# GpSimd issues the modulation loads, ScalarE the two small loads of the time mixing

## The chip, the cores and the metric

The kernel runs on one core of one Trainium2 chip. The metric is the device time of one execution in microseconds (us), and the median of several executions is compared. The core has five engines with instruction streams of their own, each executed in order: TensorE (PE, with its weight loads shown as PEld), VectorE (DVE), ScalarE (ACT), GpSimd (POOL) and SyncE (SP). SyncE computes nothing here. It only issues transfers (DMAs), each of which waits in SyncE's queue until the buffer it writes is free.

## The reference

The reference is a two-layer network on one sequence of 256 tokens with 2048 features, all in float32. Layer 0 mixes over time with an RWKV-7 recurrence, and layer 1 with chunked attention over shared keys and values. Both end in a squared-ReLU MLP with 8192 hidden features. Each sub-layer's shift, scale and gate are a product of one conditioning vector `c` with a large matrix:

```python
for layer in range(DEPTH):                                  # DEPTH = 2
    mod = c @ w_ada[layer] + b_ada[layer]                   # (1, 2048) @ (2048, 12288)
    sh1, sc1, gt1, sh2, sc2, gt2 = jnp.split(mod, 6, axis=-1)
    if layer == N_A_LAYERS:                                 # layer 1: the shared keys and values
        sh_kv, sc_kv = jnp.split(c @ w_ada_kv + b_ada_kv, 2, axis=-1)
        h_kv = modulate(rms_norm(x, g_kv), sh_kv, sc_kv)
        ...
    h = modulate(rms_norm(x, g_mix[layer]), sh1, sc1)
    y = rwkv7_time_mix(h, ...) if layer < N_A_LAYERS else chunk_band_attention(h, kp, vp, ...)
    x = x + gt1[:, None, :] * y
    h = modulate(rms_norm(x, g_mlp[layer]), sh2, sc2)
    x = x + gt2[:, None, :] * sq_relu_mlp(h, w_up[layer], w_down[layer])
return rms_norm(x, g_final)
```

Inside the time mixing, decay, in-context rate and gate come from low-rank products, whose second factors are the arrays the kernel calls `lora2`.

## The kernel before

**Weights.** Every large weight matrix is streamed from HBM in tiles of 128 x 1024 float32 (512 KB), into the rotating buffer `raw` (6 deep). For each tile `halves` writes `wH`, a rounded copy, on ScalarE (L378) and `wL`, the rest, on VectorE (L381), both 3 deep. TensorE multiplies with both halves (`proj2`, L412 and L413). One output tile of 128 features takes two `raw` tiles and 32 matmuls; below it is called a step. An MLP has 64 steps of `w_up` (activations `aHL`) and 64 of `w_down` (activations `hHL`), in four rounds of 16 and 16.

**Modulation.** The products with `c` are made on VectorE beside the matrix work: `ada_load` loads a 512 KB tile of the transposed matrix `w_ada_t`, and `ada_step` multiplies it with `c`, held in `cb`, and sums along the row (L459). Inside the MLPs and the attention the tile comes from a pool of its own, the buffer `rada`; `ada_room(n)` opens that pool, with n = 5 in an MLP and n = 3 in the attention. Everywhere else, in the time mixing above all, it is a `raw` buffer. 273 of these tiles are `rada` and 111 are `raw`. They all are used up by the end of the attention's output projection, so that the MLP of layer 1 has none.

**Time mixing.** The heads are taken as 16 pairs. The steps of up to five pairs are interleaved with the projections of the next (`proj_steps`, L819 and on). Each pair loads two small tiles, `lw` (L829, 96 KB) and `lg` (L277, 128 KB), into one buffer each.

**Who sets the order.** The program is recorded in source order, and then a scheduler arranges each engine's instructions: it may put an instruction ahead of earlier ones whose inputs are not there yet. That order is fixed when the program is built, and on the chip every engine follows its own in order. So the issuing engine of a load decides behind what else the load waits, and the built order of other engines may change with it.

Of the kernel before, what the change touches and what calls it, by code (L numbers as in the profile page):

```python
# [77 lines left out]
class Pair:  # L78
# [13 lines left out]
    def s(self, name="s", bufs=8):  # L92
        return self.b.pw.tile([P, T], F32, tag=name, bufs=bufs, name=name)
# [4 lines left out]
    @staticmethod  # L98
    def ch(t):
        return t.rearrange("p (c t) -> p c t", t=C)  # L100
# [165 lines left out]
    def late(self):  # L266
        b, nc, j, s, ch, v = self.b, self.b.nc, self.j, self.s, self.ch, self.v
        kr, ar, mk, bk, vp, u, pc, heads = self.kr, self.ar, self.mk, self.bk, self.vp, self.u, self.pc, self.heads
        pw, pp, mm = b.pw, b.pp, nc.tensor.matmul

        bank = pp.tile([P, 2, T], F32, tag="lt", bufs=2, name="lt")
        pch, py = bank[:, 0, 0:3 * C].rearrange("p (a t) -> p a t", a=3), bank[:, 1, :]
        zs = None
        for c in range(4):
            if c == 3:
                lg = pw.tile([P, 2, P], F32, tag="lg", bufs=1, name="lg")
                nc.sync.dma_start(out=lg, in_=b.d["lora2"][j, :, 2:4])  # L277
            g, sa = (pw.tile([P, C], F32, tag=n_, bufs=3, name=n_) for n_ in ("g", "sa"))
            for K in heads:
                mm(pch[K, 0, :], mk[K, c, 0:C], vp[K, c, :], start=True, stop=(c == 0))  # L280
            if c:
                for K in heads:
                    mm(pch[K, 0, :], kr[K, c, 0:C], zs[K, :], start=False, stop=True)
            nc.scalar.copy(g, pch[:, 0, :])
            yield
            for K in heads:
                mm(pch[K, 1, :], u[K, c, :], g[K, :], start=True, stop=True)
            nc.scalar.mul(sa, pch[:, 1, :], -1.0)
            yield
            for K in heads:  # L290
                mm(ch(py)[K, c, :], vp[K, c, :], mk[K, c, C:P], start=True, stop=False)
            if c:
                for K in heads:
                    mm(ch(py)[K, c, :], zs[K, :], kr[K, c, C:P], start=False, stop=False)
            for K in heads:
                ins = mm(ch(py)[K, c, :], sa[K, :], ch(ar)[K, c, :], start=False, stop=True)
            if c < 3:
                with b.tc.issue_after(ins.ins):
                    for K in heads:
                        mm(pch[K, 2, :], bk[K, 0, c, :], sa[K, :], start=True, stop=False)  # L300
                    for K in heads:
                        mm(pch[K, 2, :], bk[K, 1, c, :], vp[K, c, :], start=False, stop=True)
                zn = pw.tile([P, C], F32, tag="zs", bufs=4, name="zs")
                if c == 0:
                    nc.vector.tensor_copy(zn, pch[:, 2, :])
                else:
                    nc.vector.scalar_tensor_tensor(out=zn, in0=zs, scalar=pc[:, c, :], in1=pch[:, 2, :],
                                                   op0=ALU.mult, op1=ALU.add)
                zs = zn
            yield  # L310

        sq = self.square(py)
        yield
        var = b.psm()[:, :T]
        self.head_sums(var, sq)
        yield
        rg = s("sl", 1)
        nc.scalar.activation(rg, var, AF.Ln, scale=1.0 / C, bias=b.col(C_GN))
        nc.scalar.activation(rg, rg, AF.Exp, scale=-0.5)
        nc.vector.scalar_tensor_tensor(out=rg, in0=py, scalar=b.vec("ln_w", j), in1=rg, op0=ALU.mult, op1=ALU.mult)  # L320
        yield
        pg = b.psm()[:, :T]
        for i in range(2):
            mm(pg, lg[:, i, :], self.tg[:, i, :], start=(i == 0), stop=(i == 1))  # L324
        nc.vector.scalar_tensor_tensor(out=rg, in0=v, scalar=b.vec("ln_b", j), in1=rg, op0=ALU.add, op1=ALU.add)
        nc.vector.tensor_tensor(out=v, in0=pg, in1=rg, op=ALU.mult)
        yield


class Body:  # L330
# [27 lines left out]
            self.ada_pool = None  # L358

    def raw(self, src, shape=None, ada=False):  # L360
        if ada and self.ada_pool:
            pool, n = self.ada_pool
            t = pool.tile([P, HK * P], F32, tag="rada", bufs=n, name="rada")
        else:
            t = self.wp.tile([P, HK * P], F32, tag="raw", bufs=self.RAW_BUFS, name="raw")
        if shape is not None:
            t = t.rearrange("p (a b) -> p a b", a=shape)
        self.nc.sync.dma_start(out=t, in_=src)
        return t

    def halves(self, raw, lo=0):

        nc = self.nc
        H = self.wp.tile([P, HK, P], F32R, tag="wH", bufs=self.W_BUFS, name="wH")
        L = self.wp.tile([P, HK, P], F32R, tag="wL", bufs=self.W_BUFS, name="wL")
        Hf, Lf = (t.rearrange("p a b -> p (a b)")[:, lo:] for t in (H, L))
        raw = raw[:, lo:]
        nc.scalar.copy(Hf, raw)  # L378
        self.nhalf += 1
        eng = nc.gpsimd if self.pool_every and self.nhalf % self.pool_every == 0 else nc.vector  # L380
        eng.tensor_tensor(out=Lf, in0=raw, in1=Hf, op=ALU.subtract)  # L381
        return H, L
# [239 lines left out]
    def layer_a(self, st, sp):  # L622
        nc, tc, d = self.nc, self.tc, self.d
# [5 lines left out]
        with ExitStack() as s1:  # L629
# [9 lines left out]
            for q in range(4):  # L639
                (nc.sync if q % 2 else nc.scalar).dma_start(out=h[:, 4 * q:4 * q + 4, 1:T + 1],  # L640
                                                            in_=d["x"][:, 4 * q:4 * q + 4, :])
# [79 lines left out]
            def mixed(m, n, xx):  # L721
                t = ph.tile([P, T], F32, tag="mix", bufs=4, name="mix")
                nc.vector.scalar_tensor_tensor(out=t, in0=xx, scalar=self.vec(f"mu{m}", n),  # L723
                                               in1=h[:, n, 1:T + 1], op0=ALU.mult, op1=ALU.add)
                return t
# [26 lines left out]
            for n in range(KT):  # L752
# [19 lines left out]
                t = mixed(5, n, xx)  # L772
# [33 lines left out]
        with ExitStack() as s1:  # L806
# [12 lines left out]
            def proj_steps(pr):  # L819
                for dst, hl in (("k", xk), ("r", xr)):  # L820
                    w = self.wnext
                    src = next(weights, None)
                    self.wnext = None if src is None else self.weight(src)
                    ps = pp.tile([P, 2, T], F32, tag="pj", bufs=2, name="pj")
                    for kt in range(KT):
                        self.proj2(ps, w, lambda kt: hl[:, kt, :, 0:T], (kt, kt + 1))
                        if dst == "r" and kt == 1:
                            pr.lw = pw.tile([96, 2, P], F32, tag="lw", bufs=1, name="lw")
                            nc.sync.dma_start(out=pr.lw, in_=d["lora2"][pr.j, :96, 0:2])  # L829
                        if kt % 2 == 1:  # L830
                            if kt == KT - 1:
                                t = pw.tile([P, T], F32, tag=dst, bufs=2, name=dst)
                                nc.scalar.copy(t, ps[:, 0, :])
                                nc.vector.tensor_tensor(out=t, in0=ps[:, 1, :], in1=t, op=ALU.add)
                                setattr(pr, dst, t)
                            yield
# [363 lines left out]
```

## Time and profile before

| | us |
|---|---|
| median of 3 executions | 2736.1 (2728.79 to 2736.61) |
| the profiled execution | 2743.32 |
| its span in the trace | 2741.5 |
| layer 0, up to the time mixing | 0 to 190 |
| time mixing | 190 to 730 |
| its output projection (`out_proj`, `w_o`) | 730 to 792.5 |
| MLP of layer 0 | 792.5 to 1574.5 |
| attention and its output projection | 1574.5 to 2003.5 |
| MLP of layer 1, then the final norm | 2003.5 to 2741.5 |

The borders of the stages are the starts of the first matmuls of each (rounded for the first two). A row of a profile view names the line of the program, the engine, the instruction, what it writes and reads with buffer numbers left out, and times in us or ns. The letter q behind an engine's name marks its queue of transfers. `DVE wL L381 <- ACT wH L378` in the list of waits means that VectorE stood idle before line 381 until ScalarE had finished line 378.

### The profile page before, as it was taken

What the parts mean: (1) busy time and instruction counts of PE and PEld (TensorE: products, weight loads), DVE (VectorE), ACT (ScalarE), POOL (GpSimd) and SP (SyncE); (2) the same over time, 40 slices, a digit from 0 to 9 for tenths busy, and PEclk for the clock granted to TensorE, in tenths of its full rate; (3) what the DMA queues carried; (4) which work ended last, traced back from release to release, by engine and by line L of the source; (5) the groups of instructions that cost most, each with busy time, mean ns of one, the idle gap of its engine ahead of it and who ended that gap; (6) DMA issues with size and microseconds to landing.
All of it is one profiled execution on the core that took longest, in us unless ns stands there. A gap on an engine that the chain in (4) does not pass through costs nothing.

```text
span 2741.5 us, 55497 instructions
## 1 busy us (share of the span) xinstructions
PE 2611.7 (95%) x22154; PEld 2220.0 (81%) x22154; DVE 2093.3 (76%) x3493; ACT 1333.7 (49%) x2432; POOL 199.4 (7%) x320
## 2 busy tenths in 40 slices
PE   6998999999999999999999989999999999999997
PEld 3777777777889878887878788877898888888886
DVE  5778888889789777888878998797985555556555
ACT  3345545545446335345345454466455354453554
POOL 0002322222100000000000100000100000000002
PEclk9999999999999999999999999999999999999999
DMA  9966556566688888888888878885865555555553
GB/s 337 313 230 210 197 179 201 187 199 230 218 297 274 301 297 304 306 320 305 307 294 302 294 265 297 325 293 173 296 205 186 187 189 186 189 187 186 188 189 123
DMA packets 219251, 669.27 MB, mean 244 GB/s; under 512 B 21616, under 2 KB 69104, under 8 KB 218992
## 3 DMA queue, kind: packets, MB, share of 16 engines
q1 hardware_dynamic: 216928, 663.18, 71.4%
q8 instruction: 174, 2.85, 0.4%
q10 hardware_dynamic: 2064, 2.54, 0.3%
q14 instruction: 85, 0.70, 0.1%
HBM read 663.54 MB, written 2.10 MB: 243 GB/s over the span
## 4 chain that ended last, share of the span: by engine, by line
PE 59%; DMA 17%; DVE 14%; issue 6%; ACT 2%; SPq 0%; POOL 0%; DVEq 0%; ACTq 0%; POOLq 0%
PE pj L412 31%; PE pj L413 16%; DMA rada<-w_ada_t 10%; DVE wL L381 6%; DMA raw<-w_ada_t 5%; DVE raw L459 2%; DVE rada L459 2%; PE pj L403 1%; PE pj L401 1%; PE pj L402 1%; ACT wH L378 1%; DMA raw<-w_up 1%; PE ms L324 1%; DVE mix L723 0%; PE iv L111 0%
## 5 line engine op out<-in xcount | busy, mean ns | idle before, releaser
L412 PE MATMUL pj<-aHL,wH 128*128 128x512 f32 x3328 | 1205.0, 403 | 1.1 <-DVE v L750 0.9
L381 DVE TENSOR_TENSOR wL<-raw,wH 128x1024 fp32r<-128x1024 f32 x772 | 942.5, 1222 | 302.2 <-ACT wH L378 300.0
L378 ACT CAST wH<-raw 128x1024 fp32r<-128x1024 f32 x772 | 804.7, 1045 | 701.1 <-PE pj L412 601.3
L413 PE MATMUL pj<-aHL,wL 128*128 128x256 f32 x3328 | 940.5, 283 | 13.0 <-DVE wL L381 12.5
L412 PEld LDWEIGHTS pj<-aHL,wH 128*128 128x128 f32 x3328 | 630.5, 189 | 153.3 <-issue 9.3
L412 PE MATMUL pj<-hHL,wH 128*128 128x512 f32 x2048 | 729.0, 400 | 10.1 <-DVE hHL L963 10.1
L413 PEld LDWEIGHTS pj<-aHL,wL 128*128 128x128 f32 x3328 | 630.4, 189 | 25.7 <-DVE wL L381 23.8
L413 PE MATMUL pj<-hHL,wL 128*128 128x256 f32 x2048 | 578.6, 283 | 8.5 <-DVE wL L381 8.3
L412 PEld LDWEIGHTS pj<-hHL,wH 128*128 128x128 f32 x2048 | 387.7, 189 | 105.3 <-DVE hHL L963 11.4
L459 DVE SCALAR_TENSOR_TENSOR rada<-rada,cb 128x1024 f32<-128x1024 f32 x273 | 333.2, 1223 | 130.9 <-DMA rada<-w_ada_t 114.4
L413 PEld LDWEIGHTS pj<-hHL,wL 128*128 128x128 f32 x2048 | 389.8, 190 | 15.2 <-DVE wL L381 14.6
L509 POOL TENSOR_TENSOR ss<-ss,sq 128x256 f32<-128x256 f32 x56 | 49.4, 882 | 1642.6 <-ACT sq L508 1642.4
L988 DVE SCALAR_TENSOR_TENSOR x<-pj,mod,x 128x256 f32<-128x256 f32 x256 | 123.4, 482 | 54.5 <-PE pj L413 51.5
L459 DVE SCALAR_TENSOR_TENSOR raw<-raw,cb 128x1024 f32<-128x1024 f32 x111 | 137.9, 1247 | 29.9 <-DMA raw<-w_ada_t 29.3
L960 ACT ACTIVATE t<-t 128x256 f32<-128x256 f32 x112 | 47.0, 420 | 221.5 <-DVE t L932 221.5
L401 PE MATMUL pj<-aHL,wH 128*128 128x258 f32 x384 | 111.1, 289 | 7.1 <-DVE ks L556 4.8
L403 PE MATMUL pj<-aHL,wL 128*128 128x258 f32 x384 | 110.1, 287 | 2.7 <-DVE wL L381 2.7
L402 PE MATMUL pj<-aHL,wH 128*128 128x258 f32 x384 | 110.7, 288 | 0.0
L401 PEld LDWEIGHTS pj<-aHL,wH 128*128 128x128 f32 x384 | 74.2, 193 | 7.9 <-issue 6.0
L403 PEld LDWEIGHTS pj<-aHL,wL 128*128 128x128 f32 x384 | 75.1, 196 | 3.6 <-DVE wL L381 3.3
L402 PEld LDWEIGHTS pj<-aHL,wH 128*128 128x128 f32 x384 | 74.6, 194 | 0.1
L961 ACT ACTIVATE hHL<-t 128x256 fp32r<-128x256 f32 x128 | 53.0, 414 | 5.0 <-DVE t L556 4.5
(240 smaller groups left out, 2789.7 us busy)
## 6 DMA issues: line engine op xcount, KB each, us to landing
rada<-w_ada_t SPq DMA_DIRECT2D x273, 512.0 KB, 6.3
raw<-w_up SPq DMA_DIRECT2D x256, 512.0 KB, 4.6
raw<-w_down SPq DMA_DIRECT2D x256, 512.0 KB, 4.6
raw<-w_ada_t SPq DMA_DIRECT2D x111, 512.0 KB, 4.5
rawa<-w_ada SPq DMA_DIRECT2D x64, 512.0 KB, 7.0
raw<-w_k SPq DMA_DIRECT2D x32, 512.0 KB, 3.7
raw<-w_r SPq DMA_DIRECT2D x32, 512.0 KB, 5.1
raw<-w_o SPq DMA_DIRECT2D x32, 512.0 KB, 5.1
```

What stands on the lines that cost most here:

```text
L378: nc.scalar.copy(Hf, raw)
L381: eng.tensor_tensor(out=Lf, in0=raw, in1=Hf, op=ALU.subtract)
L401: nc.tensor.matmul(ps, H[:, i, :], a(kt)[:, 0, :], start=(first and kt == 0), stop=False)
L402: nc.tensor.matmul(ps, H[:, i, :], a(kt)[:, 1, :], start=False, stop=False)
L403: ins = nc.tensor.matmul(ps, L[:, i, :], a(kt)[:, 0, :], start=False, stop=(last and kt == KT - 1))
L412: nc.tensor.matmul(ps, H[:, i, :], a(kt), start=(kt == 0), stop=False)
L413: ins = nc.tensor.matmul(ps[:, 0, :], L[:, i, :], a(kt)[:, 0, :], start=False, stop=(kt == KT - 1))
L459: nc.vector.scalar_tensor_tensor(out=raw, in0=raw, scalar=1.0, in1=self.cb, op0=ALU.mult, op1=ALU.mult, accum_out=sums[:, n:n + 1])
L509: (eng or nc.gpsimd).tensor_tensor(out=self.ss, in0=self.ss, in1=sq, op=ALU.add)
L960: nc.scalar.activation(t, t, AF.Relu)
L961: nc.scalar.activation(h[:, 0, :], t, AF.Square)
L988: nc.vector.scalar_tensor_tensor(out=x, in0=ps[:, i, :], scalar=self.mods[(layer, 5)][:, n:n + 1], in1=x, op0=ALU.mult, op1=ALU.add)
```

## The change

Three calls change the engine that issues a transfer. `raw` keeps SyncE for weight tiles, and takes GpSimd for a tile of the pool `rada`. `lw` and `lg` are issued by ScalarE. No transfer is added, left out or changed in size, and no buffer changes.

```diff
@@ class Pair, late(): the fourth chunk
             if c == 3:
                 lg = pw.tile([P, 2, P], F32, tag="lg", bufs=1, name="lg")
-                nc.sync.dma_start(out=lg, in_=b.d["lora2"][j, :, 2:4])
+                nc.scalar.dma_start(out=lg, in_=b.d["lora2"][j, :, 2:4])
@@ class Body, raw()
     def raw(self, src, shape=None, ada=False):
+        queue = self.nc.sync
         if ada and self.ada_pool:
             pool, n = self.ada_pool
+            queue = self.nc.gpsimd
             t = pool.tile([P, HK * P], F32, tag="rada", bufs=n, name="rada")
         else:
             t = self.wp.tile([P, HK * P], F32, tag="raw", bufs=self.RAW_BUFS, name="raw")
...
-        self.nc.sync.dma_start(out=t, in_=src)
+        queue.dma_start(out=t, in_=src)
@@ class Body, layer_a(), proj_steps()
                             pr.lw = pw.tile([96, 2, P], F32, tag="lw", bufs=1, name="lw")
-                            nc.sync.dma_start(out=pr.lw, in_=d["lora2"][pr.j, :96, 0:2])
+                            nc.scalar.dma_start(out=pr.lw, in_=d["lora2"][pr.j, :96, 0:2])
```

The changed program is two lines longer from `raw` on, so L368, L378, L381 and L459 of before are L370, L380, L383 and L461 after.

The built order changes in three places. First SyncE, in the MLP of layer 0, where the `w_down` of one round gives way to the `w_up` of the next; before:

```order
L368 DMA raw<-w_down 128x1024 x3
L368 DMA rada<-w_ada_t 128x1024
L368 DMA raw<-w_down 128x1024
L368 DMA rada<-w_ada_t 128x1024
L368 DMA raw<-w_up 128x1024
L368 DMA rada<-w_ada_t 128x1024
L368 DMA raw<-w_up 128x1024 x2
```

After, over the first round and a half:

```order
L370 DMA raw<-w_up 128x1024 x32
L370 DMA raw<-w_down 128x1024 x3
L449 DMA cb<-c_row 128x1024
L370 DMA raw<-w_down 128x1024 x29
L370 DMA raw<-w_up 128x1024 x2
L449 DMA cb<-c_row 128x1024
L370 DMA raw<-w_up 128x1024 x30
```

Between the weight tiles no `rada` tile is left, only a reload of `cb` now and then.

Second GpSimd, from the end of the time mixing to the attention; `ss` is the running sum of squares of the next norm, and the memsets of `s` belong to the attention's scores. Before:

```order
L249 COPY uf_2236<-u 32x4x32 x4
L249 COPY uf_2237<-u 32x4x32 x4
L509 TENSOR_TENSOR ss<-ss,sq 128x256 x28
L1067 MEMSET s 64x64
L1068 MEMSET s 64x64
```

After (the first 14 `ss` belong to the output projection of the time mixing, the next 14 to the end of the MLP of layer 0):

```order
L370 DMA rada<-w_ada_t 128x1024 x3
L511 TENSOR_TENSOR ss<-ss,sq 128x256
L370 DMA rada<-w_ada_t 128x1024 x2
L511 TENSOR_TENSOR ss<-ss,sq 128x256
L370 DMA rada<-w_ada_t 128x1024 x2
L511 TENSOR_TENSOR ss<-ss,sq 128x256
L370 DMA rada<-w_ada_t 128x1024
L511 TENSOR_TENSOR ss<-ss,sq 128x256
L370 DMA rada<-w_ada_t 128x1024 x2
L511 TENSOR_TENSOR ss<-ss,sq 128x256
L370 DMA rada<-w_ada_t 128x1024 x231
L511 TENSOR_TENSOR ss<-ss,sq 128x256
```

The loads stand between GpSimd's sums, and 231 of them follow each other through most of the MLP of layer 0. 253 of the 273 now stand ahead of the attention's first scores.

Third VectorE, in the `w_up` of the last round of the same MLP; `t` and `hHL` are the activations of a step. Before:

```order
L459 TENSOR_SCALAR rada,ada_sums<-rada,cb 128x1024
L381 TENSOR_TENSOR wL<-raw,wH 128x1024
L963 TENSOR_TENSOR hHL<-t,hHL 128x256
L381 TENSOR_TENSOR wL<-raw,wH 128x1024
L932 TENSOR_TENSOR t<-pj,t 128x256
L459 TENSOR_SCALAR rada,ada_sums<-rada,cb 128x1024
L381 TENSOR_TENSOR wL<-raw,wH 128x1024
L963 TENSOR_TENSOR hHL<-t,hHL 128x256
L459 TENSOR_SCALAR rada,ada_sums<-rada,cb 128x1024
L381 TENSOR_TENSOR wL<-raw,wH 128x1024
```

After:

```order
L383 TENSOR_TENSOR wL<-raw,wH 128x1024
L461 TENSOR_SCALAR rada,ada_sums<-rada,cb 128x1024
L965 TENSOR_TENSOR hHL<-t,hHL 128x256
L383 TENSOR_TENSOR wL<-raw,wH 128x1024
L461 TENSOR_SCALAR rada,ada_sums<-rada,cb 128x1024
L934 TENSOR_TENSOR t<-pj,t 128x256
L383 TENSOR_TENSOR wL<-raw,wH 128x1024
L461 TENSOR_SCALAR rada,ada_sums<-rada,cb 128x1024
L965 TENSOR_TENSOR hHL<-t,hHL 128x256
L383 TENSOR_TENSOR wL<-raw,wH 128x1024
```

Here every `wL` has a modulation product beside it, where before about three of four had one. Counted over the whole order, the products up to the first late norm of this MLP (L555, after: L557) are 12 before and 17 after, up to the first residual add of the last round (L988, after: L990) 170 and 241, and up to its end 192 and 253. On TensorE 80 rows of 17,671 change place.

## The prediction

> **What bounds the kernel now.** I read the busy times by stage first, because the two MLPs do the same matrix work, 128 steps each, and only the first carries modulation tiles. The columns are span, then busy time and instructions of each engine, the granted TensorE clock, the share of time the 16 DMA engines were busy, and GB/s.
>
> ```profile
> 792.50:1574.50 782.00, 744.25 (x4229) 642.39 (x4228) 645.52 (x960) 364.55 (x548) 11.93 (x15) 0.99 0.86 300
> 1574.50:2003.50 429.00, 417.74 (x2565) 353.58 (x2563) 372.59 (x681) 222.52 (x426) 17.27 (x77) 1.00 0.79 275
> 2003.50:2729.10 725.60, 723.22 (x4227) 634.79 (x4228) 433.46 (x561) 370.21 (x548) 16.02 (x15) 1.00 0.57 182
> 190.00:730.00 540.00, 505.30 (x9330) 419.23 (x9330) 450.92 (x931) 278.64 (x750) 124.58 (x178) 0.98 0.61 197
> ```
>
> The MLP of layer 1 runs at TensorE's pace: 723 of 726 us busy. The same matmuls take 782 us in layer 0. These 56 us are the most that this stage can give. The attention leaves TensorE 11 us idle. Next I read who waits in the MLP of layer 0 (total us, times, longest).
>
> ```profile
> DVE rada L459 <- DMA rada<-w_ada_t: 86.0, 73, 3.2
> PEld pj L413 <- DVE wL L381: 35.5, 50, 2.4
> DVE wL L381 <- ACT wH L378: 29.5, 36, 1.6
> ```
>
> VectorE waits 86 us for modulation tiles, and the `wL` behind them in its order come late for TensorE. Busy time and these two waits make 645 + 86 + 30 = 761 of the 782 us: VectorE's chain sets this stage. Why the tiles are late shows in the timeline (start, duration), SyncE's queue first.
>
> ```profile
> 968.48 0.42 SPq L368 DMA_DIRECT2D rada<-w_ada_t  x1
> 972.78 3.06 SPq L368 DMA_DIRECT2D raw<-w_up  x2
> 975.90 0.42 SPq L368 DMA_DIRECT2D rada<-w_ada_t  x1
> ...
> 960.66 1.23 DVE L459 SCALAR_TENSOR_TENSOR rada<-rada,cb 128x1024 f32<-128x1024 f32 x1
> 963.78 1.23 DVE L459 SCALAR_TENSOR_TENSOR rada<-rada,cb 128x1024 f32<-128x1024 f32 x1 [0.74 <-DMA rada<-w_ada_t]
> 969.99 1.23 DVE L459 SCALAR_TENSOR_TENSOR rada<-rada,cb 128x1024 f32<-128x1024 f32 x1 [1.92 <-DMA rada<-w_ada_t]
> 973.12 1.23 DVE L459 SCALAR_TENSOR_TENSOR rada<-rada,cb 128x1024 f32<-128x1024 f32 x1
> 975.65 1.23 DVE L459 SCALAR_TENSOR_TENSOR rada<-rada,cb 128x1024 f32<-128x1024 f32 x1 [0.16 <-DMA rada<-w_ada_t]
> 983.09 1.23 DVE L459 SCALAR_TENSOR_TENSOR rada<-rada,cb 128x1024 f32<-128x1024 f32 x1 [2.83 <-DMA rada<-w_ada_t]
> 984.64 1.22 DVE L381 TENSOR_TENSOR wL<-raw,wH 128x1024 fp32r<-128x1024 f32 x1
> ...
> 985.91 0.39 PE L413 MATMUL pj<-hHL,wL 128*128 128x256 f32 x1 [1.53 <-DVE wL L381]
> ```
>
> The product at 983.09 waited 2.83 us for the load of 975.90. That load writes one of five buffers, and the product five places back had left it at 961.9 (960.66 + 1.23). For 14 us it stood behind two weight loads that waited for buffers of their own. The `wL` at 984.64 was late by that, and TensorE stood 1.53 us.
>
> **The change part by part.** *The queue of the modulation tiles.* GpSimd does next to nothing in this stage (11.9 of 782 us), so a load can now go out as soon as its buffer is free.
>
> ```profile
> L368 SPq DMA_DIRECT2D rada<-w_ada_t x273: 327/424/1089, 756.1 to 1993.7; - x137
> L459 DVE SCALAR_TENSOR_TENSOR rada<-rada,cb x273: 1205/1224/1693, 762.3 to 2000.2; 128x1024 f32<-128x1024 f32 x137
> DMA to landing us min/median/max: 4.0/6.3/8.8
> ```
>
> In the example that is 21 us ahead (983.09 − 961.9), against 4.0 to 8.8 us to landing. If nothing else changed, the 86 us of waits would go, and nearly all of the 56 us with them.
>
> *The built order.* But the scheduler uses the freedom. By the order, the products inside this MLP rise from 180 (192 less 12) to 236 (253 less 17), and 224 of them stand ahead of the last `w_down` round, where 158 did. That is 66 more in the first seven eighths, and 12 instead of 22 in the last. The attention loses them. So I take the seven eighths apart: 684 us before (7/8 of 782), and 635 at TensorE's pace (7/8 of 725.6). VectorE: 565 busy (7/8 of 645.5), plus 66 x 1.22 = 81, makes 646, and with its wait for `wH` (7/8 of 29.5 = 26) 672 us. DMA: 205 MB (7/8 of 300 GB/s x 782 us) plus 66 x 0.524 MB = 240 MB. The rates which this chip reached with such tiles are:
>
> ```profile
> 1700.00:1800.00 100.00, 97.44 (x571) 82.73 (x570) 80.80 (x128) 47.32 (x80) 0.46 (x4) 1.00 0.88 320
> 1690.00:1700.00 10.00, 9.82 (x59) 8.42 (x58) 6.95 (x11) 4.55 (x8) 0.00 (x0) 1.00 0.96 342
> 1760.00:1770.00 10.00, 10.00 (x60) 8.76 (x59) 7.71 (x12) 4.35 (x7) 0.00 (x0) 1.00 0.99 379
> ```
>
> 320 GB/s over 100 us gives 750 us, 342 at share 0.96 gives 702, 379 at 0.99 gives 633. With its own queue full at all times the rate should lie between the last two; I take 355, which gives 676. VectorE's 672 and the DMA's 676 both stand above TensorE's 635, so 676: **−8 us**, with ends at −38 (VectorE's 646 without a wait) and +66.
>
> The last eighth has few products: 97.8 to TensorE's 90.7, **−7**. The products fetched forward from the attention use its three buffers instead of five. There a tile takes at least (6.3 landing + 1.22 product + 0.42 issue)/3 = 2.65 us, and the 37 of the last `w_up` round 98 us, against 97 of the 676 that fall on that round: **+1**. With 8.8 us to landing it would be 3.48 us each, 129 us, +32; I take the median, since nothing but their own kind is queued ahead of them.
>
> *The attention* has 72 products before and 20 after.
>
> ```profile
> DVE rada L459 <- DMA rada<-w_ada_t: 28.3, 25, 4.5
> ```
>
> Most of this wait goes, but TensorE was idle for only 11.3 us there, which is the upper end; the lower is zero. I take half, **−6**.
>
> *The output projection before the MLP* has 5 more products by the order (17 for 12), 5 x 1.22 = 6 us of VectorE; some of it lies beside TensorE's work: **+2** of 0 to +6.
>
> *The time mixing.* ScalarE takes over 32 loads.
>
> ```profile
> 0.77 0.43 ACTq L575 DMA_DIRECT2D ct<-c  x1
> SPq L277 <- PE lt L287: 15.5, 8, 5.4
> SPq L829 <- PE ms L128: 4.1, 5, 1.1
> DVE raw L459 <- DMA raw<-w_ada_t: 29.3, 32, 2.6
> ```
>
> The first row is what an issue costs ScalarE: 0.43 x 32 = 13.8 us of its queue, beside 279 busy of 540, so part of it is hidden by idle time; each stands ahead of small copies on which the pair's next matmuls wait. In return SyncE no longer holds weight and modulation loads behind `lg` and `lw` for 20 us, of which VectorE's 29.3 us of waits could give some back. Ends −13 and +14; I take **+3**, nearer to zero because both sides lie beside other work.
>
> Sum: −8 −7 +1 −6 +2 +3 = −15. The profiled execution took 2743.3 us (span 2741.5), so it would take 2728.3; it lies 7.2 above the median of the three timed runs, 2736.1, and on that footing the forecast is **2721 us**. About 0.3%, 8 us, is what a measurement of this kernel can tell from no change.
>
> **The rivals.** *Transfers bind (slower).* The seven eighths turn from a gain to a loss that eats the other −7 where the 240 MB come at less than 347 GB/s (240/691). Between 345 and 320 GB/s they take 695 to 750 us, and the sum is +4 to +59; in the middle +30, or 2766 us. For it: 320 is the best that any 100 us of this kind of work has shown, and the products now stand between every two `wL`, so each late tile stops TensorE's weights. Against it: so far SyncE's queue, not the engines, held the loads back.
>
> *GpSimd's issuing holds up VectorE (slower).* A row shows that the two engines can collide.
>
> ```profile
> 778.64 1.22 DVE L381 TENSOR_TENSOR wL<-raw,wH 128x1024 fp32r<-128x1024 f32 x1
> 781.30 1.77 DVE L381 TENSOR_TENSOR wL<-raw,wH 128x1024 fp32r<-128x1024 f32 x1
> 781.25 0.74 POOL L509 TENSOR_TENSOR ss<-ss,sq 128x256 f32<-128x256 f32 x1 [8.13 <-ACT sq L508]
> ```
>
> Beside a GpSimd sum the same operation took 0.55 us longer. If each load's issue did that, 224 x 0.55 = 123 us would lie on VectorE's 672, and the kernel would come to about 2840. It decides from (691 − 672)/224 = 0.08 us a load. No trace here has a load from GpSimd, so this price runs from zero to 0.55; I take zero, since the sum reads and writes whole tiles of 128 x 256, which an issue does not. The Trainium skill (SBUF — State Buffer, "Who interferes with whom") says that a VectorE instruction with two SBUF inputs collides with a GpSimd instruction that reads SBUF, and infers that making descriptors needs only the write side. The row agrees with the first half; by the second this rival's price is zero too.
>
> *No change.* The wait moves from the queue to the transfer: at about 347 GB/s the stage stays at its 782 us and the rest cancels, 2736. The Trainium skill (DMA: Bandwidth & Descriptors, "Issuing engines are not separate DMA queues") says that starting DMAs on several engines saves only the sequencer's time to start them. By that the change would save SyncE's 273 x 0.424 = 116 us, which are on no path. The trace speaks against it with the 14 us in which the load at 975.90 was held by order alone.
>
> *All the waits go.* At 379 GB/s and with `wH` in time, VectorE's 646 sets the seven eighths, 30 below what I take: 2691.
>
> **How the numbers follow.** Forecast 0.33, all waits gone 0.13, no change 0.14, transfers bind 0.25, VectorE held up 0.15. Faster by over 0.3%: 0.46, within: 0.14, slower: 0.40. The forecast's own range is 2700 to 2727. The whole range starts at 2688, just past the case without waits, and ends at 2785, which takes in most of the binding transfers (to 2795) and the small end of the holding-up; beyond it are some 0.15 above and 0.04 below.
>
> **What would show it.** In the trace of after, the MLP of layer 0 should take 760 to 778 us at 338 to 348 GB/s, with VectorE near 715 us busy there; VectorE's waits for `rada` should fall well below 86 us in spite of 56 more products, and a load should go out within a microsecond of the product that frees its buffer. The attention should take 420 to 427 us, the time mixing 540 to 545. A row of L383 with a mean above 1.25 us in the MLP would speak for the holding-up, waits for `rada` above 86 us at a DMA share over 0.95 for the binding transfers. The reasoning is wrong if the stage gets faster though the waits stay, or if the tiles land later than 8.8 us while the DMA engines stand idle.

## The result and the profile after

| | before | after |
|---|---|---|
| median of 4 executions, us | 2736.36 (2728.79 to 2736.65) | 2713.77 (2709.22 to 2717.43) |
| ratio, 95% interval | | 0.9923 [0.9900, 0.9946] |
| the profiled execution (its span), us | 2743.32 (2741.5) | 2709.22 (2707.5) |
| up to the MLP of layer 0 | 792.5 | 791.0 |
| MLP of layer 0 | 782.0 | 763.1 |
| attention and its output projection | 429.0 | 414.2 |
| MLP of layer 1 | 725.6 | 724.6 |
| final norm to the end | 12.4 | 14.6 |

The kernel became 0.8% faster. A second measurement of it on another chip, told below, gave 0.9879 [0.9855, 0.9903]. Of the 34 us between the two spans, 18.9 lie in the MLP of layer 0 and 14.8 in the attention. The stage times are those of single profiled executions: that of before took 7.0 us more than its median and that of after 4.6 less than its own, so the spans lie 11.5 us further apart than the medians, which differ by 22.6. One execution told below, the profiled one of behind_sp, took 11336 us, over four times as long as the others of its kernel, and is in no ratio and no stage time.

The busy times of the stages after (stretch, length, busy time of PE, PEld, DVE, ACT and POOL, granted clock, DMA share, GB/s): the MLP of layer 0, the attention, the MLP of layer 1, then the time mixing (up to a rounded border), the first seven eighths of the MLP of layer 0, a stretch inside it, and its last `w_up` round.

```profile
791.00:1554.10 763.10, 735.24 (x4229) 640.73 (x4228) 703.85 (x1079) 367.94 (x549) 137.56 (x252) 0.99 0.93 347
1554.10:1968.30 414.20, 412.01 (x2563) 351.75 (x2563) 307.63 (x552) 221.93 (x427) 30.20 (x98) 1.00 0.60 205
1968.30:2692.90 724.60, 722.50 (x4228) 634.45 (x4226) 431.34 (x559) 368.92 (x546) 15.47 (x14) 1.00 0.56 181
190.00:728.00 538.00, 507.11 (x9363) 421.39 (x9363) 453.38 (x936) 280.98 (x754) 130.47 (x182) 0.99 0.62 200
791.00:1459.30 668.30, 644.26 (x3716) 562.27 (x3715) 618.20 (x963) 319.27 (x479) 119.22 (x225) 0.99 0.95 358
1172.00:1260.50 88.50, 87.12 (x498) 75.89 (x497) 84.36 (x132) 51.54 (x89) 17.46 (x33) 1.00 1.00 387
1355.00:1459.30 104.30, 95.67 (x514) 81.74 (x513) 87.39 (x135) 50.58 (x88) 18.50 (x35) 0.95 0.92 340
```

VectorE does 58 us more in the MLP (704 for 646) and 65 us less in the attention (308 for 373), because the products moved. TensorE, with the same 4229 matmuls in the MLP, shows 735 us busy for 744, and it is idle for 28 us instead of 38.

The waits inside the MLP of layer 0 after:

```profile
DVE rada L461 <- DMA cb<-c_row: 28.4, 7, 4.7
PEld pj L415 <- DVE wL L383: 25.0, 16, 4.3
PE pj L415 <- DVE wL L383: 19.8, 12, 4.0
DVE rada L461 <- DMA rada<-w_ada_t: 15.8, 19, 3.1
```

VectorE's waits for modulation tiles fell from 86.0 us to 15.8. In their place stands one that the prediction did not have: 28.4 us in 7 waits for a new half of `c`. All halves share one buffer, SyncE still issues their load, and it takes 7.1 us from issue to landing (median of 13).

The handing over, from the timeline after (start, duration), and the groups of the two instructions in question (busy, mean ns):

```profile
901.04 1.22 DVE L461 SCALAR_TENSOR_TENSOR rada<-rada,cb 128x1024 f32<-128x1024 f32 x1
902.56 0.53 POOL L370 DMA_DIRECT2D rada<-w_ada_t  x1 [2.15 <-DVE rada L461]
...
L383 DVE TENSOR_TENSOR wL<-raw,wH 128x1024 fp32r<-128x1024 f32 x772 | 943.1, 1222 | 356.6 <-ACT wH L380 352.1 <-DMA raw<-w_o 1.6 <-PE o L405 0.4
L370 POOL DMA_DIRECT2D rada<-w_ada_t x273 | 145.4, 533 | 682.0 <-DVE rada L461 636.1 <-DVE aHL L564 28.5 <-PE S L1073 6.1
```

A load goes out 0.3 us after the product that frees its buffer (902.56 against 901.04 + 1.22). GpSimd had stood waiting for that.

### The profile page after: what moved, and what is told of

Same layout as the page of the kernel before. It is cut to its first block, busy times and chain, and to the rows that moved or that the text cites. A ratio compares the mean times of both kernels' runs of the same rounds, so it can differ in the third digit from the quotient of the medians.

```text
span 2707.5 us, 55672 instructions
## 1 busy us (share of the span) xinstructions
PE 2596.7 (96%) x22154; PEld 2215.5 (82%) x22154; DVE 2088.7 (77%) x3493; ACT 1334.1 (49%) x2432; POOL 350.2 (13%) x593
## 4 chain that ended last, share of the span: by engine, by line
PE 63%; issue 13%; DVE 12%; DMA 6%; ACT 2%; POOL 2%; SPq 0%; DVEq 0%; POOLq 0%; ACTq 0%
PE pj L414 33%; PE pj L415 16%; DVE wL L383 4%; DMA raw<-w_ada_t 3%; DVE rada L461 2%; POOL rada L370 2%; DMA cb<-c_row 2%; PE pj L404 2%; PE pj L405 2%; PE pj L403 2%; DVE raw L461 1%; PE iv L111 1%; PE ms L324 1%; ACT wH L380 1%; DVE x L919 1%
## 5 line engine op out<-in xcount | busy, mean ns | idle before, releaser
L383 DVE TENSOR_TENSOR wL<-raw,wH 128x1024 fp32r<-128x1024 f32 x772 | 943.1, 1222 | 356.6 <-ACT wH L380 352.1
L380 ACT CAST wH<-raw 128x1024 fp32r<-128x1024 f32 x772 | 803.7, 1043 | 720.8 <-PE pj L414 611.9
L414 PEld LDWEIGHTS pj<-aHL,wH 128*128 128x128 f32 x3328 | 632.7, 190 | 156.1 <-issue 10.3
L461 DVE SCALAR_TENSOR_TENSOR rada<-rada,cb 128x1024 f32<-128x1024 f32 x273 | 331.2, 1217 | 49.0 <-DMA cb<-c_row 32.9
L370 POOL DMA_DIRECT2D rada<-w_ada_t x273 | 145.4, 533 | 682.0 <-DVE rada L461 636.1
L990 DVE SCALAR_TENSOR_TENSOR x<-pj,mod,x 128x256 f32<-128x256 f32 x256 | 123.2, 481 | 53.6 <-PE pj L415 50.7
L461 DVE SCALAR_TENSOR_TENSOR raw<-raw,cb 128x1024 f32<-128x1024 f32 x111 | 137.9, 1246 | 25.4 <-DMA raw<-w_ada_t 25.2
```

The lines of the kernel that those rows point to most:

```text
L370: queue.dma_start(out=t, in_=src)
L414: nc.tensor.matmul(ps, H[:, i, :], a(kt), start=(kt == 0), stop=False)
L461: nc.vector.scalar_tensor_tensor(out=raw, in0=raw, scalar=1.0, in1=self.cb, op0=ALU.mult, op1=ALU.mult, accum_out=sums[:, n:n + 1])
L990: nc.vector.scalar_tensor_tensor(out=x, in0=ps[:, i, :], scalar=self.mods[(layer, 5)][:, n:n + 1], in1=x, op0=ALU.mult, op1=ALU.add)
```

## The experiments

Kernels under one heading ran in one group on one chip (behind_sp on one of its own), against the kernel before on that chip, whose median was 2736 to 2747 us there. Whole times are compared as ratios. The stage times are those of one profiled execution each; the two of the changed kernel agree within 1 us (763.1 and 763.3, 414.2 and 413.3).

| kernel | ratio to before | MLP of layer 0, us | attention, us |
|---|---|---|---|
| small_only | 0.9986 [0.9971, 1.0001] | 783.7 | 431.2 |
| rada_only | 0.9883 [0.9863, 0.9904] | 760.4 | 415.9 |
| tied_sp | 0.9996 [0.9981, 1.0010] | 781.2 | 425.3 |
| tied_pool | 0.9803 [0.9779, 0.9827] | 726.0 | 419.7 |
| mlp_only | 0.9919 [0.9899, 0.9939] | 761.4 | 424.5 |
| attn_only | 1.0096 [1.0069, 1.0123] | 785.9 | 456.5 |
| cb_kept | 0.9831 [0.9807, 0.9854] | 752.3 | 412.3 |
| rada_act | 0.9957 [0.9939, 0.9975] | 772.9 | 426.8 |
| late_sp | 1.0005 [0.9988, 1.0022] | 775.4 | 435.9 |
| tied_cb | 0.9793 [0.9766, 0.9819] | 721.5 | 429.5 |
| after_again | 0.9879 [0.9855, 0.9903] | 763.3 | 413.3 |
| behind_sp | 0.9862 [0.9837, 0.9886] | not read | not read |

### The two halves of the change, and the queue without the moved products

**small_only** is before with `lw` and `lg` on ScalarE:

```diff
-                nc.sync.dma_start(out=lg, in_=b.d["lora2"][j, :, 2:4])
+                nc.scalar.dma_start(out=lg, in_=b.d["lora2"][j, :, 2:4])
...
-                            nc.sync.dma_start(out=pr.lw, in_=d["lora2"][pr.j, :96, 0:2])
+                            nc.scalar.dma_start(out=pr.lw, in_=d["lora2"][pr.j, :96, 0:2])
```

> Only lw and lg go to ScalarE; the modulation tiles stay with SyncE, so the built order of VectorE in the MLP of layer 0 is that of before. If the gain belongs to the modulation tiles, this kernel is within 4 us of before (2736), and its time mixing (190 to 730 in before) is within 3 us. If the small loads bring part of it by freeing SyncE, it is 5 to 10 us faster than before, all of it ahead of 792 us, with less than 29 us of VectorE's waits for raw<-w_ada_t.

**rada_only** is before with only the modulation tiles on GpSimd:

```diff
+        queue = self.nc.sync
         if ada and self.ada_pool:
             pool, n = self.ada_pool
+            queue = self.nc.gpsimd
...
-        self.nc.sync.dma_start(out=t, in_=src)
+        queue.dma_start(out=t, in_=src)
```

> Only the modulation tiles go to GpSimd; lw and lg stay with SyncE. If they make the whole gain: 18 to 27 us faster than before, the MLP of layer 0 near 763 us and the attention near 414, as with the full change. If the small loads make a third or more: at most 15 us faster than before.

The small loads brought 0.14%, with an interval that just holds no change; the modulation tiles alone brought as much as the whole change (0.9883, against 0.9879 in its second measurement), some 32 us, more than the 18 to 27 that were expected.

Two further kernels keep the products where the source puts them. Each product takes, in place of the constant 1.0, a column of ones that ScalarE makes from the sums of its own step. So no product can be put ahead of its step. **tied_sp** is before with this, **tied_pool** is after with it, so the two also differ in the small loads.

```diff
-        nc.vector.scalar_tensor_tensor(out=raw, in0=raw, scalar=1.0, in1=self.cb, ...
+        nc.vector.scalar_tensor_tensor(out=raw, in0=raw, scalar=1.0 if self.one is None else self.one, in1=self.cb, ...
...
+    def tie(self, ps):
+        if self.ada_pool:
+            self.one = self.ada_pool[0].tile([P, 1], F32, tag="one", bufs=4, name="one")
+            self.nc.scalar.activation(self.one, ps, AF.Identity, scale=0.0, bias=self.col(C_ONE))
```

> Before, with SyncE issuing, but every modulation product takes a column of ones that ScalarE makes from the sums of its own step, so the scheduler can't put a product ahead of its step. It is the control of tied_pool: 128 small ScalarE operations in an MLP, 175 products in the MLP of layer 0 instead of 192. All theories: 2725 to 2760 us, VectorE's waits for rada 50 us or more in the MLP of layer 0.

> The same columns of ones with GpSimd issuing the modulation tiles and ScalarE the small ones: 175 products in the MLP of layer 0, as in tied_sp, so no work moves from the attention into the MLP. If the free queue by itself makes the gain: 20 to 45 us faster than tied_sp, nearly all in the MLP of layer 0, whose waits for rada fall below 20 us and which comes to 735 to 755 us. If the gain came from the products that the scheduler moved out of the attention: within 8 us of tied_sp, since none are moved here.

With the products at the same places (172 in the MLP of layer 0, 81 in the attention and 17 in the MLP of layer 1, in both traces) the queue is worth 2685.6 − 2738.6 = −53 us of span, nearly all of it in the MLP of layer 0 (781.2 to 726.0). That is more than the 20 to 45 us that were expected. The expectation of 50 us or more of waits for `rada` in tied_sp was wrong: VectorE waits for no modulation tile in that MLP. Other loads are held up there, as two lists of waits show: of SyncE's queue, then of ScalarE.

```profile
SPq L368 <- DVE rada L459: 335.3, 114, 6.8
SPq L368 <- DVE hHL L964: 138.4, 48, 5.5
SPq L368 <- DVE wL L381: 85.1, 45, 5.6
```

```profile
ACT wH L378 <- DMA raw<-w_down: 88.0, 41, 4.5
ACT wH L378 <- PE pj L412: 87.6, 60, 4.4
ACT wH L378 <- DMA raw<-w_up: 66.9, 41, 3.9
```

SyncE stood 335 us in 114 waits for a product to free a modulation buffer, and the weight tiles behind those waits came late: ScalarE waited 155 us for them. The same lists of tied_pool:

```profile
SPq L370 <- DVE wL L383: 502.6, 193, 7.3
SPq L370 <- DVE t L934: 96.6, 50, 2.7
SPq L370 <- DVE hHL L966: 28.4, 11, 3.1
```

```profile
ACT wH L380 <- PE pj L414: 159.8, 134, 2.5
ACT wH L380 <- issue: 60.3, 39, 1.7
```

No wait of ScalarE for a raw tile is left, and the stage runs at TensorE's pace (726.0, against 725.6 before and 724.6 after for the MLP of layer 1, which has no modulation there). In the kernel before, the same queue held things up the other way round: SyncE's longest waits in this MLP were for buffers of weights.

```profile
SPq L368 <- DVE wL L381: 368.0, 163, 6.5
...
SPq L368 <- DVE rada L459: 3.0, 2, 1.9
```

There the modulation loads stood behind the weight loads, and VectorE waited 86 us. Both orders of one queue came to nearly the same time, 2738.6 and 2741.5 us of span; why they agree so closely, no run shows.

In the changed kernel the scheduler pulls products forward: 242 lie in the MLP of layer 0, 20 in the attention and none behind. Beside tied_pool its MLP is 37 us longer (763.1 for 726.0), its attention 5.5 shorter, and the stages ahead of and behind the two 10 shorter together. Its span is 22 us above tied_pool's (2707.5 for 2685.6).

### One room at a time, the row c, and another engine

**mlp_only** issues from GpSimd in the rooms of five buffers alone, **attn_only** in the room of three alone; the small loads are on ScalarE in both. The second room of five, which the program opens for the MLP of layer 1, holds the last 20 of these loads. They go out during the attention's output projection, from GpSimd in mlp_only and from SyncE in attn_only.

```diff
-            queue = self.nc.gpsimd
+            queue = self.nc.gpsimd if n == 5 else self.nc.sync      # attn_only: n == 3
```

> Part of the change alone: GpSimd issues the modulation loads in the two rooms of five buffers, which span the MLP of layer 0; SyncE issues them in the room of three, which spans the attention behind it (and the last round of that MLP). The products' places through the first seven eighths of the MLP are those of the changed kernel. Theory (the attention became shorter because products were taken out of it, not because of the queue): the MLP about 760 us, the attention 414 to 420, ratio to before 0.989 to 0.995. Rival (the attention's 15 us come from GpSimd's issuing in it): the MLP about 763, the attention 425 to 430, ratio 0.996 to 0.999.

> The other part alone: SyncE issues the modulation loads in the two rooms of five buffers, GpSimd in the room of three. The products stand where they stood before. Theory (products taken out): the MLP 780 to 784 us as before, the attention 421 to 428, ratio 0.996 to 1.000. Rival (the queue): the attention about 414, ratio 0.993 to 0.996.

mlp_only had all of the gain in the MLP. The attention fell between the two expectations, to 424.5. It has 32 products, where before had 82 and after has 20; of the 30 loads that go out in it, SyncE issues 10 and GpSimd the 20 of the output projection. With that it lost 4.5 of the 14.8 us. The other 10.3 come with 12 products fewer, no load from SyncE and a granted clock of 1.00 for 0.99, which these runs do not separate.

attn_only went against both theories: the attention took 27.5 us more than before. Some 7 us of that can be the granted clock, 0.981 for 0.996 (an estimate: the missing share times the length). The waits in a stretch of its projections of v (1690 to 1820 us), where before had 1.3 us of this kind on PE; the two rows tell of the same 12 waits:

```profile
PEld m L1052 <- DVE vf L934: 19.7, 12, 2.4
PE m L1052 <- DVE vf L934: 15.9, 12, 2.1
```

VectorE's built order there, before and in attn_only:

```text
1882 L459 TENSOR_SCALAR rada,ada_sums<-rada,cb 128x1024
1883 L381 TENSOR_TENSOR wL<-raw,wH 128x1024
1884 L459 TENSOR_SCALAR rada,ada_sums<-rada,cb 128x1024
1885 L381 TENSOR_TENSOR wL<-raw,wH 128x1024
1886 L932 TENSOR_TENSOR vf<-pj,vf 128x256
```

```text
1910 L461 TENSOR_SCALAR rada,mod_3_79<-rada,cb 128x1024
1911 L383 TENSOR_TENSOR wL<-raw,wH 128x1024
1912 L461 TENSOR_SCALAR rada,mod_3_79<-rada,cb 128x1024 x2
1913 L934 TENSOR_TENSOR vf<-pj,vf 128x256
```

With the loads on GpSimd the scheduler puts one or two products right ahead of 11 of the 16 sums `vf`, on which TensorE's next transposition waits; before had none there. In tied_pool GpSimd issues in the attention too, no product stands right ahead of a `vf`, and the attention took 419.7. So it is the order built for the queue that costs here, and not GpSimd's issuing. In the changed kernel the last `vf` is at 1740.9 us and the first of the 20 products left in the attention at 1886.2.

**cb_kept** is after with both halves of `c` kept in the MLP's rooms, and four modulation buffers there in place of five:

```diff
-                s2.enter_context(self.ada_room(5))
+                s2.enter_context(self.ada_room(4))
...
+        if self.cbs is not None and i in self.cbs:
+            self.cb = self.cbs[i]
+            return
```

> The changed kernel, but in the two rooms of the MLP both halves of the broadcast row c stay in SBUF, so that VectorE has no reload of cb to wait for there; for their space the rooms have four modulation buffers in place of five. Theory (VectorE is full where the products crowd, so the 28 us that it waits for cb in the MLP of layer 0 are on the path): ratio to before 0.980 to 0.988, the MLP 742 to 755 us, waits for cb under 10 us. Rival (the transfers are what is full there, so that another wait takes their place): ratio 0.988 to 0.996, the MLP 758 to 768, VectorE's wait for modulation tiles up by 15 us or more.

The MLP became 10.8 us shorter than in the changed kernel (752.3 for 763.1), with fewer waits of both kinds:

```profile
DVE rada L476 <- DMA cb<-c_row: 14.7, 3, 6.0
DVE rada L476 <- DMA rada<-w_ada_t: 11.4, 12, 1.7
```

The wait for `c` shrank by 13.7 us, to 14.7 and not under the 10 that were expected, and the stage by 10.8. So the new wait was on the path, and the transfers did not take its place; one buffer fewer cost nothing that shows.

**rada_act** is after with `self.nc.scalar` in place of `self.nc.gpsimd`.

> ScalarE issues the modulation loads in place of GpSimd. An issue waits for a product to free its buffer, and ScalarE's rounding of weights and its MLP steps stand behind it. Theory (the gain comes from a queue with nothing behind its waits, which ScalarE isn't): ratio to before 0.998 to 1.03, TensorE idle in the MLP of layer 0 more than the 28 us of the changed kernel. Rival (the gain is only SyncE being relieved, of issue time and of waits, so any other queue does): ratio 0.986 to 0.996.

0.9957 lies just inside the rival's range and outside the theory's: another queue was worth about 0.4% even where ScalarE's own work stands behind its waits. It is clearly less than GpSimd's, and TensorE is idle 36 us in the MLP (772.9 − 736.8) for 28. What of the rest is ScalarE's blocking and what the other order (230 products in the MLP for 242) was not separated.

### The wait taken off SyncE

**late_sp** is tied_sp with two loads ahead in place of four:

```diff
-        while self.ada_pool and len(self.ada_q) < self.ada_pool[1] - 1 and self.ada_load():
+        while self.ada_pool and len(self.ada_q) < max(2, self.ada_pool[1] - 3) and self.ada_load():
```

> The tied kernel with SyncE's queue, in which SyncE waits 335 us in 114 waits of the MLP of layer 0 for a modulation product to free its buffer. Here a modulation load is asked for only when two loads are ahead, not four: with five buffers it then goes into one whose product is three products back, so the same queue issues the same loads and hardly waits. Theory (what costs time is the weight loads that stand behind such a wait on the same queue): SyncE's waits for products in that MLP under 80 us, the MLP 730 to 755 us, ratio to before 0.980 to 0.991. Rival (SyncE's issue time, or two queues in place of one, is the gain): the MLP 770 to 785, ratio 0.996 to 1.002.

It did not do what it was meant to. The scheduler built nearly the same order of issues for SyncE, and SyncE waited about as long as in tied_sp:

```profile
SPq L368 <- DVE rada L459: 315.6, 111, 7.0
```

So its unchanged time says nothing on the cause. **tied_cb** and **after_again** ran beside it.

> The tied kernel with GpSimd's queue, and both halves of c kept in the MLP's rooms, with four modulation buffers in each. Theory (VectorE is 637 of 726 us busy there and TensorE idle 4, so VectorE's 13 us of waiting for cb are off the path): ratio to before 0.978 to 0.984, the MLP of layer 0 723 to 729 us. Rival (waits for cb cost wherever they are, as in the changed kernel): ratio 0.970 to 0.977, with the MLP and the output projection before it shorter by 8 us or more.

> The changed kernel itself, on the chip of the two others, so that its ratio has an interval of the same make: ratio 0.986 to 0.995. Beside the tied kernel's 0.980 it tells whether the products moved into the MLP cost (theory: it stays at least 0.006 above the tied one) or not (rival: within 0.003).

tied_cb (0.9793) is not distinguishable from tied_pool (0.9803), so VectorE's waits for `c`, 13.3 us in tied_pool's MLP of layer 0, cost nothing that the whole time shows. The stages leave it less clear: that MLP is 4.5 us shorter in tied_cb, and its attention 9.8 longer at a granted clock of 0.98 for 1.00. Both are the fastest kernels here, ahead of before and after. The changed kernel stays 0.0086 above tied_cb in this group, and rada_only 0.0080 above tied_pool in the first, though a product with its column of ones takes longer (1281 ns for 1215, medians of tied_pool and after). So the products moved into the MLP do cost.

**behind_sp** is tied_sp with three things changed together: the modulation loads of the rooms keep their places in the program, the MLPs ask for their weights three output tiles (six `raw` tiles) ahead, and in the rooms of five one modulation load is asked for ahead in place of four (the last lines are for `w_up`; `w_down` is treated alike):

```diff
-        self.nc.sync.dma_start(out=t, in_=src)
+        ins = self.nc.sync.dma_start(out=t, in_=src)
+        if ada and self.ada_pool:
+            self.tc.keep_in_program_order(ins)
...
-        while self.ada_pool and len(self.ada_q) < self.ada_pool[1] - 1 and self.ada_load():
+        while self.ada_pool and len(self.ada_q) < (2 if self.ada_pool[1] < 5 else 1) and self.ada_load():
...
+        def fill():
+            while srcs and len(ahead) < 3:
+                src = srcs.popleft()
+                ahead.append([self.raw(src[:, i * HK * P:(i + 1) * HK * P]) for i in range(KT // HK)])
...
-            w = self.weight(d["w_up"][layer, q * KT + f])
+            w = next_weight()
```

> The tied kernel with SyncE's queue once more, and the same loads on the same queue, but in the MLP of layer 0 each modulation load is now held behind weight loads that are asked for three tiles ahead. By the order of the program the product that frees its buffer then stands, in most cases, at or ahead of the VectorE step that the weight load before it waits for, instead of some three steps behind. Theory (the loss is the weight loads that stand on SyncE behind a wait for a product): SyncE's waits for products in that MLP fall from 335 to under 150 us, ScalarE's waits for raw weights from 155 to under 70, the MLP from 781 to 730 to 760, ratio to before 0.979 to 0.992. Rival (two queues issue better than one, or SyncE's issue time is the cost, wherever it waits): the MLP 770 to 785, ratio 0.995 to 1.003. If the waits for products stay above 250 us, it tells nothing.

The ratio is that of four executions (2694.8 to 2697.6 us). The trace is of the fifth, and it can't tell how long SyncE waits in these.

The time speaks for the theory: one queue, SyncE's, with the same loads in an order in which it should hardly wait for products, wins 0.0134 (0.9996 − 0.9862) of the 0.0193 that lie between tied_sp and tied_pool; the kernels ran in different groups. SyncE issues as many loads as in tied_sp, so two thirds of the gain can be had without a second queue and without taking any issue time off SyncE. That the waits for products are gone was planned from the built order and is not shown, and what the weight loads' new places, or fewer modulation loads ahead, did by themselves was not tried.

## Why the prediction was right, and where its steps were not

**The queue as the cause.** Right. VectorE's waits for modulation tiles, the wait that the example stood for, fell from 86.0 to 15.8 us, and rada_only shows that the issuing engine of the modulation loads by itself makes the gain. With the products fixed the queue is worth 53 us, close to the 56 that the prediction named for the case that "nothing else changed". But there the block ran the other way, from the modulation loads to the weights, so that the two figures lie so close is luck.

**The built order takes part of it back.** Right in kind: the changed kernel's span is 31 us below tied_sp's (2738.6 − 2707.5), where tied_pool's is 53 below it. The total was not met by errors that cancel: each of the three parts that follow came out faster than was said. By medians 2713.8 us was measured for 2721, by the profiled executions 2709.2 for 2728.3.

**The MLP of layer 0, −8 −7 +1 = −14.** Measured −18.9. The sum split the 782 us of before evenly; by its rounds they were 679.6 and 102.4 (the last `w_down` starts at 1472.1). So the seven eighths lost 11.3 where −8 and +1 were said, and the last eighth 7.6 where −7 was said. The seven eighths took 668.3 us where 676 was said, at 358 GB/s where 355 was taken. The number fits, the reason less so: the rate was not a limit of the transfers. Full DMA engines moved 387 GB/s in the stretch above, 8% more, and before already had 394 for 10 us in this very MLP (1185 to 1195), above the 379 that the prediction took for the most. VectorE filled the stretch: it was busy for 618.2 of the 668.3 us, where the sum had 646, and its longest waits there were these, with which it comes to 663.

```profile
DVE rada L461 <- DMA cb<-c_row: 28.4, 7, 4.7
DVE rada L461 <- DMA rada<-w_ada_t: 14.2, 18, 3.1
DVE wL L383 <- ACT wH L380: 2.4, 4, 1.1
```

The sum gave VectorE 26 us of waits for `wH` and none for `c`; it was 2.4 and 28.4. With 13.7 us of the latter gone, cb_kept did the stage in 752.3. With fewer products in the stage tied_pool went at TensorE's pace. Of the 26 us that are left between them (752.3 − 726.0), 23 lie in two rounds (cb_kept, then tied_pool):

```profile
1251.80:1456.10 204.30, 188.35 (x1026) 162.22 (x1025) 174.74 (x268) 87.54 (x127) 35.39 (x67) 0.95 0.94 344
1250.30:1431.70 181.40, 179.98 (x1026) 157.08 (x1025) 158.08 (x229) 94.01 (x160) 25.33 (x48) 1.00 0.94 331
```

All of cb_kept's waits for `c` and for tiles (14.7 and 11.4 us) lie there, and the granted clock is 0.95 for 1.00. What each of them costs is open. The last `w_up` round, on three buffers, took 104.3 where the same round took 97.9 before: +6.4 for the +1, inside its bound of +32. Its granted clock was 0.95 for 1.00, but rada_only took 102.1 for it at 1.00.

**The attention, −6.** This is the step that was mis-sized; it was −14.8, beyond what was called the upper end. (The products in it were 81 by the order, 273 less 192, and 82 in the trace, where 72 was said.) The bound took TensorE's 11.3 idle us as all that could be won and its busy time as fixed. The busy time fell too, from 417.7 to 412.0 for the same matmuls, and the idle time to 2.2. The MLP shows it as well: 744.3 busy before, 735.2 after, 722.3 in tied_pool. Part of that is the granted clock, 0.987, 0.989 and 1.000 there; less the missing share times the length it is 734, 727 and 722 (an estimate), and 416 and 412 in the attention. So a busy TensorE in these records holds some of its waiting.

**Output projection and time mixing, +2 and +3.** All up to the MLP came to −1.5. The last matmul of the time mixing itself (L324) starts at 723.4 us for 729.1 before, so the mixing became 5.7 us shorter and the rest up to the MLP 4.2 longer (67.6 for 63.4). Over the other profiled kernels the end of the mixing varies by more than that, so the sign of the first is not shown. The small loads cost nothing that small_only could show; the larger end (+14) did not come.

**The rivals.** *Transfers bind* turned on 347 GB/s; 358 over the seven eighths and 387 over 88.5 us put it out. *GpSimd holds up VectorE* turned on 0.08 us a load; `wL` took 1222 ns in the mean before and after. Of the whole tiles after, 220 ran beside an issue and no other work of GpSimd, with a mean of 1217 ns, and 474 beside nothing of GpSimd, with 1223; beside a GpSimd sum `ss` it was 1278 (49). So the price of an issue was zero. The Trainium skill (SBUF — State Buffer, "Who interferes with whom") inferred as much, and this trace agrees. *No change* needed the transfers to stay at about 347 GB/s in the seven eighths, or the issue time to be all that a second queue saves. The first did not come (358), and tied_sp against tied_pool refutes the second here by 53 us. The Trainium skill (DMA: Bandwidth & Descriptors, "Issuing engines are not separate DMA queues") speaks of issue time alone, and the measurement decides against it where an issue waits for a buffer. *All the waits go*, 2691, is 0.9835 of before; tied_pool went below it with 0.9803, by another way: its waits went because the products stayed where they were.

## What to carry to other kernels

Two kinds of loads whose buffers are freed by different work do not belong in one engine's queue when one of them can wait long: read the queue's own waits, and see who stands behind the longest. A scheduler that sees loads come sooner moves the work that uses them, so cost the new order, and try the change with the order held fixed: with the loads on GpSimd the fixed order was the faster one here. Don't take TensorE's busy time in a trace as a floor; take the same matmuls in a stage that waits for nothing, at the same granted clock. Look at the clock before you put a slow round down to a queue.

## What the hardware showed that was not expected

The 16 DMA engines held 387 GB/s for 88.5 us at a share of 1.00, and in cb_kept 398 for 100 us (963 to 1063); the best 100 us before had 339 (5 to 105). A load from GpSimd took 0.53 us of its queue and landed after 6.3 us (median of 273), just as one from SyncE before (0.42 us of its queue and 6.3 us), and `wL` on VectorE took no longer beside it.
